# Batch normalisation with fixed statistics: even and odd channels as tiles, and transfers that no longer wait their turn

## The chip, the cores and the metric

The kernel runs on one core of a Trainium2 chip. The metric is the device time of one execution in microseconds (us); lower is better. The profile is of one such execution. Its span runs from the first to the last instruction, and is a little shorter than the device time.

## The reference

The input x has the shape 32 x 256 x 128 x 128 (images, channels, height, width) in float32. Each channel has a gamma, a beta, a mean and a variance, which are given:

```python
return gamma * (x - mean) / np.sqrt(var + eps) + beta
```

For each channel this is one multiplication and one addition per element, with scale = gamma / sqrt(var + eps) and shift = beta - mean * scale. The input is 536.87 MB, the output as much, and each element is used once.

## The kernel before

**Tiles.** An image has 256 channels and a tile has 128 partitions, so the work is 64 tiles (NT = 64), two per image: channels 0 to 127, then 128 to 255 (lines 40 and 41). A partition holds one channel of one image, 16,384 elements or 65,536 bytes, contiguous in HBM. A tile is 8 MiB, contiguous in HBM as well. Three buffers in SBUF, `bufs[0..2]`, take the tiles in turn, and a tile is computed in place.

**Loads.** SyncE (SP) issues all loads, in order, on one DMA queue (q1 in the profile). Tile 0 comes in two pieces: the left quarter of its columns (line 84), then four small loads of the parameters (line 87), then the other three quarters (line 91). For each later tile (lines 92 to 100), SyncE waits until the store that last used the buffer has landed (line 97). From tile 2 on it also waits until the load before has landed (line 100, attached to the instruction of line 98), and only then issues the load. So the load queue holds one transfer at a time.

**Parameters.** Each vector of 256 values is loaded into 16 partitions of `rows`. VectorE (DVE) transposes `rows` in blocks of 32 x 32 into `turned` (line 104), and four small copies (line 109) place the values in `par`, one channel per partition, with one column for each half of the channels. ScalarE (ACT) takes the square root (line 111), and VectorE computes `scale_t` and `shift_t` (lines 118 to 121). These are 128 x 2: column `i % 2` serves tile i.

**Compute.** One TENSOR_SCALAR of VectorE per tile (line 126) waits for the load and multiplies and adds in place. Tile 0 is computed in two pieces. The last tile is divided: VectorE takes its first 9216 columns, ScalarE the rest (line 154).

**Stores.** ScalarE issues all stores, in order, on a queue of its own (q10). Before store i it waits until store i - 1 has landed (`turn_of_store`, lines 140 and 141), and the store itself waits for the compute (line 138). So the store queue holds one transfer at a time too. The last store has no such wait for the one before. At the end SyncE waits for all stores (line 164).

SyncE, ScalarE and VectorE each work through their instructions in program order. An instruction that waits holds up all behind it on its engine.

Of the kernel before, what the change touches and what calls it, by code (L numbers as in the profile page):

```python
# [8 lines left out]
NBUF = 3  # L9
# [4 lines left out]
@with_exitstack  # L14
def kernel(
    ctx: ExitStack,
    tc: tile.TileContext,
    x: bass.AP,
    gamma: bass.AP,
    beta: bass.AP,  # L20
    running_mean: bass.AP,
    running_var: bass.AP,
    out: bass.AP,
):
    nc = tc.nc
    eps = 1e-5
    f32 = mybir.dt.float32

    N, C, H, W = x.shape
    P = nc.NUM_PARTITIONS  # L30
    assert C % P == 0
    NCB = C // P
    HW = H * W
    NT = N * NCB
    B = 32
    NQ = P // B
    NE = 16
    NPAR = 4

    xr = x.rearrange("n (cb p) h w -> (n cb) p (h w)", p=P)  # L40
    outr = out.rearrange("n (cb p) h w -> (n cb) p (h w)", p=P)

    params = ctx.enter_context(tc.tile_pool(name="params", bufs=1))
    data = ctx.enter_context(tc.tile_pool(name="data", bufs=1))
    bufs = [data.tile([P, HW], f32, name=f"t{s}", tag=f"t{s}") for s in range(NBUF)]
    rows = params.tile([B, NPAR * C], f32, name="rows", tag="rows")
    turned = params.tile([B, NPAR * C], f32, name="turned", tag="turned")
    par = params.tile([P, NPAR, NCB], f32, name="par", tag="par")
    eps_t = params.tile([P, 1], f32, name="eps_t", tag="eps")
    std_t = params.tile([P, NCB], f32, name="std_t", tag="std")  # L50
    rstd_t = params.tile([P, NCB], f32, name="rstd_t", tag="rstd")
    scale_t = params.tile([P, NCB], f32, name="scale_t", tag="scale")
    ms_t = params.tile([P, NCB], f32, name="ms_t", tag="ms")
    shift_t = params.tile([P, NCB], f32, name="shift_t", tag="shift")

    loaded = [tc.alloc_semaphore(f"loaded{s}") for s in range(NBUF)]
    stored = [tc.alloc_semaphore(f"stored{s}") for s in range(NBUF)]
    early = tc.alloc_semaphore("early")  # L60
    done = tc.alloc_semaphore("done")
    fetched = tc.alloc_semaphore("fetched")
    vec = tc.alloc_semaphore("vec")
    act = tc.alloc_semaphore("act")

    with tc.tile_critical():  # L66
        count = [0]

        def step(inst, sem=None, value=None):

            if sem is not None:
                inst._wait_ge(sem, value)
            elif count[0]:
                inst._wait_ge(vec, count[0])
            inst.then_inc(vec, 1)
            count[0] += 1
            return count[0]

        left, right = slice(0, HW // 4), slice(HW // 4, HW)
        last = NT - 1  # L80

        nc.sync.dma_start(out=bufs[0][:, left], in_=xr[0][:, left]).then_inc(early, 16)
        zeroed = step(nc.vector.memset(rows[:], 0.0))  # L85
        for r, ap in enumerate((running_var, gamma, beta, running_mean)):
            inst = nc.sync.dma_start(out=rows[0:NE, r * C : (r + 1) * C], in_=ap.partition_broadcast(NE))  # L87
            if r == 0:
                inst._wait_ge(vec, zeroed)
            inst.then_inc(fetched, 16)  # L90
        nc.sync.dma_start(out=bufs[0][:, right], in_=xr[0][:, right]).then_inc(loaded[0], 16)  # L91
        for i in range(1, NT):
            s, turn = i % NBUF, i // NBUF


            if turn:
                nc.sync.wait_ge(stored[s], 16 * turn)
            inst = nc.sync.dma_start(out=bufs[s][:], in_=xr[i]).then_inc(loaded[s], 16)
            if i >= 2:
                inst._wait_ge(loaded[(i - 1) % NBUF], 16 * ((i - 1) // NBUF + 1))  # L100


        step(nc.vector.memset(eps_t[:], eps))  # L103
        step(nc.vector.transpose(out=turned[:], in_=rows[:]), fetched, 16 * NPAR)  # L104

        blocks = turned.rearrange("p (rc q b) -> p rc q b", q=NQ, b=B)
        flat = par.rearrange("p r cb -> p (r cb)")
        for q in range(NQ):
            placed = step(nc.vector.tensor_copy(out=flat[q * B : (q + 1) * B], in_=blocks[:, :, q, 0]))  # L109
        var_t, gamma_t, beta_t, mean_t = (par[:, r] for r in range(NPAR))  # L110
        nc.scalar.activation(  # L111
            out=std_t[:],
            in_=var_t,
            func=mybir.ActivationFunctionType.Sqrt,
            bias=eps_t[:],
            scale=1.0,
        )._wait_ge(vec, placed).then_inc(act, 1)
        step(nc.vector.reciprocal(out=rstd_t[:], in_=std_t[:]), act, 1)  # L118
        step(nc.vector.tensor_mul(out=scale_t[:], in0=gamma_t, in1=rstd_t[:]))  # L119
        step(nc.vector.tensor_mul(out=ms_t[:], in0=mean_t, in1=scale_t[:]))  # L120
        ready = step(nc.vector.tensor_sub(out=shift_t[:], in0=beta_t, in1=ms_t[:]))  # L121
        nc.vector.wait_ge(vec, ready)

        def compute(i, cols=slice(0, HW)):
            t, cb = bufs[i % NBUF], i % NCB
            return nc.vector.tensor_scalar(  # L126
                out=t[:, cols],
                in0=t[:, cols],
                scalar1=scale_t[:, cb : cb + 1],
                scalar2=shift_t[:, cb : cb + 1],  # L130
                op0=mybir.AluOpType.mult,
                op1=mybir.AluOpType.add,
            ).then_inc(done, 1)

        def store(i, after):
            s = i % NBUF
            inst = nc.scalar.dma_start(out=outr[i], in_=bufs[s][:]).then_inc(stored[s], 16)
            inst._wait_ge(done, after)

        def turn_of_store(i):  # L140
            nc.scalar.wait_ge(stored[(i - 1) % NBUF], 16 * ((i - 1) // NBUF + 1))

        compute(0, left)._wait_ge(early, 16)
        compute(0, right)._wait_ge(loaded[0], 16)
        store(0, 2)
        for i in range(1, last):
            compute(i)._wait_ge(loaded[i % NBUF], 16 * (i // NBUF + 1))
            turn_of_store(i)
            store(i, i + 2)

        turns = last // NBUF + 1
        compute(last, slice(0, VCOLS))._wait_ge(loaded[last % NBUF], 16 * turns)
        t, cb = bufs[last % NBUF], last % NCB
        nc.scalar.activation(  # L154
            out=t[:, VCOLS:],
            in_=t[:, VCOLS:],
            func=mybir.ActivationFunctionType.Identity,
            bias=shift_t[:, cb : cb + 1],
            scale=scale_t[:, cb : cb + 1],
        )._wait_ge(loaded[last % NBUF], 16 * turns).then_inc(done, 1)  # L160
        store(last, last + 3)

        for s in range(NBUF):
            nc.sync.wait_ge(stored[s], 16 * ((NT - s + NBUF - 1) // NBUF))
# [30 lines left out]
```

## Time and profile before

| | us |
|---|---|
| median of 3 runs | 2488.96 |
| lowest, highest | 2486.43, 2489.02 |
| the profiled execution's own time | 2486.43 |
| its span | 2484.7 |
| VectorE busy | 564.0 |
| ScalarE busy | 7.9 |
| a load or a store of 8 MiB, from issue to landing | 38.6 |
| first store issued | 30.04 |
| last load landed, last store issued | 2454.41, 2460.82 |

All profile lines are from the profiled execution. A busy time is the time that an engine spent in instructions; waiting and issuing DMAs do not count. In a line of the chain of waits, the first number is the start in us from the start of the span, the second the length. "A <- B: total, times, longest" in a list of waits says that A stood for B, in us. In a group line, "8.31 <-DMA t<-in_x_dram" in brackets is the engine's idle time just before, and what ended it. DMA digits are tenths of the 16 DMA engines' time in 40 slices of the span, where 9 is 90% or more.

### The profile page before, as it was taken

What the parts mean: (1) busy time and instruction counts of PE and PEld (TensorE: products, weight loads), DVE (VectorE), ACT (ScalarE), POOL (GpSimd) and SP (SyncE); (2) the same over time, 40 slices, a digit from 0 to 9 for tenths busy, and PEclk for the clock granted to TensorE, in tenths of its full rate; (3) what the DMA queues carried; (4) which work ended last, traced back from release to release, by engine and by line L of the source; (5) the groups of instructions that cost most, each with busy time, mean ns of one, the idle gap of its engine ahead of it and who ended that gap; (6) DMA issues with size and microseconds to landing.
All of it is one profiled execution on the core that took longest, in us unless ns stands there. A gap on an engine that the chain in (4) does not pass through costs nothing.

```text
span 2484.7 us, 389 instructions
## 1 busy us (share of the span) xinstructions
DVE 564.0 (23%) x76; ACT 7.9 (0%) x3; POOL 0.2 (0%) x4
## 2 busy tenths in 40 slices
DVE  3121221212212222122221221212212122121221
ACT  0000000000000000000000000000000000000001
POOL 0000000000000000000000000000000000000000
DMA  9999999999999999999999999999999999999999
GB/s 422 423 439 434 430 436 435 437 428 437 435 436 432 433 438 429 436 434 431 434 427 437 437 426 439 436 432 430 436 438 430 433 427 438 430 430 437 436 426 406
DMA packets 18707, 1073.84 MB, mean 432 GB/s; under 512 B 2128, under 2 KB 2192, under 8 KB 2192
## 3 DMA queue, kind: packets, MB, share of 16 engines
q1 hardware_dynamic: 9488, 536.94, 50.1%
q10 hardware_dynamic: 9216, 536.88, 49.9%
q14 instruction: 3, 0.02, 0.0%
HBM read 536.94 MB, written 536.87 MB: 432 GB/s over the span
## 4 chain that ended last, share of the span: by engine, by line
DMA 99%; ACT 0%; SPq 0%; issue 0%; DVE 0%; DVEq 0%
DMA t<-in_x_dram 99%; ACT t L154 0%; SPq L87 0%; DVE rows L85 0%; SPq L91 0%; DVE eps_t L103 0%; DVEq L190 0%; SPq L66 0%
## 5 line engine op out<-in xcount | busy, mean ns | idle before, releaser
L126 DVE TENSOR_SCALAR t<-t,scale_t,shift_t 128x16384 f32<-128x16384 f32 (+2 forms) x65 | 560.5, 8624 | 1886.5 <-DMA t<-in_x_dram 1886.4
L154 ACT ACTIVATE t<-t,shift_t,scale_t 128x7168 f32<-128x7168 f32 x1 | 6.4, 6361 | 2442.7 <-DMA t<-in_x_dram 2442.7
L104 DVE STREAM_TRANSPOSE turned<-rows 32x1024 f32<-32x1024 f32 x1 | 1.2, 1233 | 7.1 <-DMA rows<-in_running_mean_dram 7.1
L111 ACT ACT_TABLE_LOAD x1 | 1.3, 1283 | 0.9 <-SPq L66 0.9
L85 DVE MEMSET rows<- 32x1024 f32 x1 | 0.9, 912 | 1.2 <-SPq L66 1.2
L109 DVE COPY par<-turned 32x8 f32<-32x8 f32 x4 | 0.6, 162 | 0.1
L111 ACT ACTIVATE std_t<-par,eps_t 128x2 f32<-128x2 f32 x1 | 0.3, 295 | 9.2 <-DVE par L109 9.2
L118 DVE RECIPROCAL rstd_t<-std_t 128x2 f32<-128x2 f32 x1 | 0.2, 166 | 0.4 <-ACT std_t L111 0.4
L121 DVE TENSOR_TENSOR shift_t<-par,ms_t 128x2 f32<-128x2 f32 x1 | 0.2, 163 | 0.0
L120 DVE TENSOR_TENSOR ms_t<-par,scale_t 128x2 f32<-128x2 f32 x1 | 0.2, 161 | 0.0
L119 DVE TENSOR_TENSOR scale_t<-par,rstd_t 128x2 f32<-128x2 f32 x1 | 0.2, 161 | 0.0
L179 POOL MEMSET const-bfloat16-1.0<- 128x1 bf16 x1 | 0.1, 102 | 0.0
L179 POOL MEMSET const-uint8-127<- 128x1 uint8 x1 | 0.1, 101 | 0.0
L179 POOL MEMSET const-float32-0.0<- 128x1 f32 x1 | 0.1, 99 | 0.2 <-issue 0.2
L179 POOL MEMSET const-float32-1.0<- 128x1 f32 x1 | 0.1, 98 | 0.0
L103 DVE MEMSET eps_t<- 128x1 f32 x1 | 0.1, 59 | 0.1
## 6 DMA issues: line engine op xcount, KB each, us to landing
t<-in_x_dram SPq DMA_DIRECT2D x1, 6144.0 KB, 19.4
t<-in_x_dram SPq DMA_DIRECT2D x1, 2048.0 KB, 7.6
out_dram<-t ACTq DMA_DIRECT2D x64, 38.6
t<-in_x_dram SPq DMA_DIRECT2D x63, 38.6
rows<-in_running_var_dram SPq DMA_DIRECT2D x1, 16.0 KB, 6.4
rows<-in_gamma_dram SPq DMA_DIRECT2D x1, 16.0 KB, 6.2
rows<-in_beta_dram SPq DMA_DIRECT2D x1, 16.0 KB, 5.9
rows<-in_running_mean_dram SPq DMA_DIRECT2D x1, 16.0 KB, 5.9
```

What stands on the lines that cost most here:

```text
L85: zeroed = step(nc.vector.memset(rows[:], 0.0))
L103: step(nc.vector.memset(eps_t[:], eps))
L104: step(nc.vector.transpose(out=turned[:], in_=rows[:]), fetched, 16 * NPAR)
L109: placed = step(nc.vector.tensor_copy(out=flat[q * B : (q + 1) * B], in_=blocks[:, :, q, 0]))
L111: nc.scalar.activation(out=std_t[:], in_=var_t, func=mybir.ActivationFunctionType.Sqrt, bias=eps_t[:], scale=1.0,)._wait_ge(vec, placed).t ...
L118: step(nc.vector.reciprocal(out=rstd_t[:], in_=std_t[:]), act, 1)
L119: step(nc.vector.tensor_mul(out=scale_t[:], in0=gamma_t, in1=rstd_t[:]))
L120: step(nc.vector.tensor_mul(out=ms_t[:], in0=mean_t, in1=scale_t[:]))
L121: ready = step(nc.vector.tensor_sub(out=shift_t[:], in0=beta_t, in1=ms_t[:]))
L126: return nc.vector.tensor_scalar(out=t[:, cols], in0=t[:, cols], scalar1=scale_t[:, cb : cb + 1], scalar2=shift_t[:, cb : cb + 1], op0=myb ...
L154: nc.scalar.activation(out=t[:, VCOLS:], in_=t[:, VCOLS:], func=mybir.ActivationFunctionType.Identity, bias=shift_t[:, cb : cb + 1], scale ...
L179: nc = _bacc.Bacc("TRN2", target_bir_lowering=False, num_devices=1)
```

## The change

Tile i now holds the even channels of an image (i even) or the odd ones (i odd), so partition p holds channel 2p or 2p + 1. The rows of a tile are 65,536 bytes as before, but lie 131,072 bytes apart in HBM, for loads and stores alike. The parameters follow: one more VectorE copy, of 32 x 1024 elements, puts the even channels before the odd ones in a new tile `lined`, which is transposed in place of `rows`.

The two rules of one transfer at a time are dropped. A load now waits only for the store that frees its buffer, and a store only for its compute. The three buffers, the split of the first and the last tile, the queues and the order of the issues stay.

```diff
-    xr = x.rearrange("n (cb p) h w -> (n cb) p (h w)", p=P)
-    outr = out.rearrange("n (cb p) h w -> (n cb) p (h w)", p=P)
+    xv = x.rearrange("n (p cb) h w -> n cb p (h w)", cb=NCB)
+    outv = out.rearrange("n (p cb) h w -> n cb p (h w)", cb=NCB)
+    xr = [xv[i // NCB, i % NCB] for i in range(NT)]
+    outr = [outv[i // NCB, i % NCB] for i in range(NT)]
...
+    lined = params.tile([B, NPAR * C], f32, name="lined", tag="lined")
...
+            inst = nc.sync.dma_start(out=bufs[s][:], in_=xr[i]).then_inc(loaded[s], 16)
             if turn:
-                nc.sync.wait_ge(stored[s], 16 * turn)
-            inst = nc.sync.dma_start(out=bufs[s][:], in_=xr[i]).then_inc(loaded[s], 16)
-            if i >= 2:
-                inst._wait_ge(loaded[(i - 1) % NBUF], 16 * ((i - 1) // NBUF + 1))
+                inst._wait_ge(stored[s], 16 * turn)
...
-        step(nc.vector.transpose(out=turned[:], in_=rows[:]), fetched, 16 * NPAR)
+        step(
+            nc.vector.tensor_copy(
+                out=lined.rearrange("b (r cb p) -> b r cb p", r=NPAR, cb=NCB),
+                in_=rows.rearrange("b (r p cb) -> b r cb p", r=NPAR, cb=NCB),
+            ),
+            fetched,
+            16 * NPAR,
+        )
+        step(nc.vector.transpose(out=turned[:], in_=lined[:]))
...
         def store(i, after):
             s = i % NBUF
-            inst = nc.scalar.dma_start(out=outr[i], in_=bufs[s][:]).then_inc(stored[s], 16)
-            inst._wait_ge(done, after)
-        def turn_of_store(i):
-            nc.scalar.wait_ge(stored[(i - 1) % NBUF], 16 * ((i - 1) // NBUF + 1))
+            nc.scalar.dma_start(out=outr[i], in_=bufs[s][:])._wait_ge(done, after).then_inc(stored[s], 16)
...
-            turn_of_store(i)
             store(i, i + 2)
```

## The prediction

> **What bounds the kernel now.** I read the shares of busy time first, then the DMA part, then the chain of work that ended last, then SyncE's own waits, and last the head and the tail in order of time.
>
> ```profile
> DVE 564.0 (23%) x76; ACT 7.9 (0%) x3; POOL 0.2 (0%) x4
> ...
> DMA  9999999999999999999999999999999999999999
> ...
> q1 hardware_dynamic: 9488, 536.94, 50.1%
> q10 hardware_dynamic: 9216, 536.88, 49.9%
> ...
> DMA 99%; ACT 0%; SPq 0%; issue 0%; DVE 0%; DVEq 0%
> ```
>
> VectorE is busy for less than a quarter of the span. The two DMA queues, loads on q1 and stores on q10, together took 50.1 + 49.9 = 100.0% of the time of the 16 DMA engines. So no engine ever stands still long enough to be seen, and the chain is 99% DMA. The question is therefore not whether a ring waits, but whether a DMA engine does.
>
> ```profile
> 247.22 38.65 DMA t<-in_x_dram
> ...
> 1214.33 38.80 DMA t<-in_x_dram
> ...
> 1253.15 39.06 DMA t<-in_x_dram
> ...
> 1601.49 39.35 DMA t<-in_x_dram
> ...
> 2377.15 38.62 DMA t<-in_x_dram
> ```
>
> These are pieces of the chain: start, length, what. One load of 8 MiB takes 38.6 us because a store of 8 MiB shares the engines with it. The shortest piece is 38.62. In the trace's packet records one row of 65,536 bytes takes 2.418 us, load or store, and an engine starts the next row 2.414 us after the last one. A tile and its store are 16 rows per engine, 16 x 2.414 = 38.62: the shortest piece is an engine that never pauses. Sixty-four such tiles cost 64 x 38.62 = 2471.7 us. The span of 2484.7 is only 13.0 above that. Of the 13.0, the periods between load 1 (landed at 52.87) and load 63 (landed at 2454.41, seen as the ACTIVATE's start at 2454.43) hold 2401.56 - 62 x 38.62 = 7.1 us. The rest is head (first row at about 2.0 us) and tail (last store landed at 2483.4).
>
> The 7.1 us lie in a few stretches, such as pieces of 38.80, 39.06 and 39.35. The packet records say whose they are: the load rows took 5.2 us per engine more than 2.418 each over the run, the store rows 0.1. So what this kernel still loses is mostly a slow read of HBM now and then, and not a ring without work.
>
> ```profile
> SPq L98 <- DMA t<-in_x_dram: 1378.8, 62, 48.0
> SPq L97 <- DMA out_dram<-t: 1009.0, 61, 16.8
> ```
>
> SyncE issues load i, then waits 1009.0 / 61 = 16.5 us for the store that frees the next buffer (line 97), then another 1378.8 / 62 = 22.2 us for load i itself to land (line 98), and issues load i+1.
>
> **The change, part by part.**
>
> *The load's wait for the load before goes (line 100 of before, shown under line 98).* Each load can then be issued when its buffer is free, some 22 us earlier, and lies in the load ring when the one before ends. Removed: 62 waits of 22.2 us of SyncE, whose only other work is the next issue (0.33 us each). What is late next is the wait for the store, and that is over 22 us before the load ring needs work. Gain on the path: in before, the load ring is empty for a moment at each change of load (from issue to first row; at the start the first issue is at 0.95 and the first row at 1.98, so about 1 us, or a little over a packet with the landing). But in this moment the store ring has the engine alone and moves two of its rows in the time of one (the last store, alone, takes 19.3 us where 38.6 is the rule). The engine loses nothing, and the store gets back later what it lent. So the gain is 0. If this cover were gone (both rings empty at once), a gap would cost about 1 us, 62 of them 62 us; the 100.0% rules that out in before, and the chain's own excess of 7.1 us bounds it.
>
> *The store's wait for the store before goes (line 141, turn_of_store).* A load lands, its compute takes 8.81 us, and the store before lands 16.5 us after the load. So the store is issued 16.5 - 8.8 = 7.7 us earlier and lies queued. Behind it on ScalarE's queue there are only later stores, and the last tile's ACTIVATE, which waits for its load. By the same reasoning the gain is 0.
>
> *Both rings now always hold work.* Loads run at 38.62 per tile, and buffers come free in time: load i+3 needs store i, which lands 16.5 us after load i+1, or 22 us before load i+2 ends. The order of the two streams stays as it is, so the tail does too: store 62 is still moving when the last compute ends (now 2460.8; the engines work throughout), and the last store goes alone for 19.3 us. Change: 0.
>
> *Parameters: one more VectorE copy.* The copy of 32x1024 with a stride of two elements is not in the trace. Below, the 32x1024 MEMSET took 0.91 us; above, I take two of the STREAM_TRANSPOSE of that shape, 2 x 1.23 = 2.5 us. I take 1.2, the single transpose, which also reads and writes 1024 elements. All of it delays the first compute, which has this cover:
>
> ```profile
> 12.61 2.41 DVE L126 TENSOR_SCALAR t<-t,scale_t,shift_t 128x4096 f32<-128x4096 f32 x1
> 23.33 6.68 DVE L126 TENSOR_SCALAR t<-t,scale_t,shift_t 128x12288 f32<-128x12288 f32 x1 [8.31 <-DMA t<-in_x_dram]
> ```
>
> VectorE stands 8.31 us before the second piece of tile 0 lands. Even 2.5 us goes into it: cost 0. The cover would have to shrink below 2.5 for the copy to move store 0 (30.04). The four parameter loads are issued as before.
>
> *Rows 128 KiB apart instead of 64 KiB.* Each partition still reads or writes 65,536 contiguous bytes, one packet, so packet count and size stay the same: 128 rows for each transfer. SBUF's side is unchanged. In HBM a tile is now every second row of 16 MiB. The trace shows no such pattern, so I bound it by the rows there are. Lowest: all excess goes, 62 periods of 38.62, -7.1 us. Highest: each period is like the worst piece, 39.35 against the present mean of 2401.56 / 62 = 38.735, so 62 x 0.615 = +38 us. Between them lies the stretch at 1136 to 1292 us (38.88, 39.01, 38.80, 39.06; mean 38.94), 62 x 0.20 = +12.6 us. I take 0, since the nearest row is the present load itself: same packet, same engines, and 99 of 100 packets at 2.418.
>
> The Trainium skill speaks against this edit: the page "DMA: Bandwidth & Descriptors", section "Latency and other measured facts", says that copies whose per-partition rows lie a large power of two apart in HBM lose rate, 207 GB/s each way at 512 KiB against 214 at full rate, and far less from 2 MiB up. By its figure for 512 KiB the sum would be 214 / 207 = 1.034 times the time, an estimate of some 2570 us; the page has no figure for 128 KiB, and the trace of before, at 64 KiB, shows about 217 each way (8.39 MB in 38.65 us), no loss.
>
> **Sum.** Load ring 0, store ring 0, tail 0, copy 0, row distance 0 (-7.1 to +38). Against the profiled execution (2486.43, span 2484.7) that is 2486.4. This execution is the lowest of the three shown, whose median is 2488.96, 0.1% above; I place the forecast between the two, at 2488.
>
> **Rivals.**
>
> *No change (the forecast), chance 0.60.* The rings are never empty and the engines as full as before. For it: 100.0% and the 38.62 floor. It covers 2484 to 2494, the median +- 0.2% (about what a measurement of this kernel can tell from no change).
>
> *Slower by reads of HBM, chance 0.26.* The place is the load packet, which already has nearly all of the lengthening (5.2 against 0.1 us per engine). If the wider rows make the slow stretch the rule, 38.94 per tile, the time is 2488 + 12.6 = 2501; if all are like the worst piece, 2526. It decides from a mean period of 38.735 + 5 / 62 = 38.82 on. For it: the slow stretches involve most engines at once, so they come from something that the engines share (the records show up to 16 load rows lengthened within 3 us). Against it: each row is still read as one contiguous packet, and most periods show no trace of a limit.
>
> *Faster, chance 0.14.* The wider rows, or the rings that run without pause, take the slow stretches away: 2488 - 7.1 = 2481. For it: nothing in the trace says that 64 KiB is the best distance for reads. Against it: the waits removed do not coincide with the slow stretches, which come at irregular times. Less than 2480 would need rows faster than 2.414 us, which the trace never shows.
>
> *The change does not do what it says.* If stores landed too late, loads would still go out only as the one before lands, and the time would be 2488 as well; the 22 us speak against it. This is inside the first case.
>
> Left out at the top are the slow cases beyond 2503, about 1 in 10, and at the bottom 1 in 30. So the range is 2480 to 2503; the likeliest case alone has 2484 to 2494.
>
> **What would show it.** SyncE's waits should show one line, for stores, and no longer a wait for the load before. Issue to landing of a load should rise from 38.6 to about 38.6 + 22 = 61 us without the kernel being slower, since part of it is queueing; that of a store to about 46. VectorE's idle time before the second piece of tile 0 should fall to about 7. The sum of the two queues should stay at 100%, and the pieces between loads at 38.62 to 38.7. I am wrong if pieces of 38.9 or more are the rule (reads), if the sum of the queues falls under 99% (a ring without work), or if the last store no longer starts with the engines busy.

## The result, and the profile after

| | before | after |
|---|---|---|
| median of 4 runs each, same chip, us | 2487.69 | 2508.43 |
| lowest, highest | 2485.97, 2489.02 | 2507.63, 2509.33 |
| the profiled execution, its span | 2486.43, 2484.7 | 2507.63, 2505.8 |
| last load landed | 2454.41 | 2475.11 |
| last store issued, landed | 2460.82, 2483.39 | 2481.52, 2504.09 |

The changed kernel is slower: the ratio is 1.0084, with a 95% interval of 1.0066 to 1.0101. The forecast was no change, at 2488, with a range to 2503. The runs of some kernels below (waits at every second tile, three passes, two pieces with waits) fall into a faster and a slower group, so for these the spread is given, and for the first two the ratio leaves out the slowest runs.

The table already says where the time is. The last load lands 20.70 us later. From there on the two kernels are alike: 6.41 us to the issue of the last store in both, and 22.57 us to its landing in both. So the whole loss is in the date of the last load. The page of the kernel after:

```profile
GB/s 420 432 432 430 431 426 435 433 432 433 434 433 434 433 433 433 433 430 426 431 433 432 425 434 433 434 430 427 434 435 430 425 434 434 433 424 433 433 433 320
...
q1 hardware_dynamic: 9488, 536.94, 49.9%
q10 hardware_dynamic: 9216, 536.88, 49.6%
...
another core or an unknown queue 75%; DVE 22%; DMA 2%; ACT 0%; issue 0%; SPq 0%; ACTq 0%; DVEq 0%
...
out_dram<-t ACTq DMA_DIRECT2D x64, 49.7
t<-in_x_dram SPq DMA_DIRECT2D x63, 58.5
```

Three lines matter. The queues sum to 99.5% instead of 100.0%: 0.5% of 2505.8 is 12.5 us per engine without a packet. The last slice moved 320 GB/s, where before it was 406. And the chain no longer says DMA 99%. The rates of the kernel before, for the last slice:

```profile
GB/s 422 423 439 434 430 436 435 437 428 437 435 436 432 433 438 429 436 434 431 434 427 437 437 426 439 436 432 430 436 438 430 433 427 438 430 430 437 436 426 406
```

That the chain follows "another core or an unknown queue" here only means that a load was issued long before the wait that it ends, so the profile ties nothing to it; one core runs. A load takes 58.5 us from issue to landing and a store 49.7, both mostly queueing. SyncE's own waits in the kernel after:

```profile
SPq L98 <- DMA out_dram<-t: 2390.5, 61, 67.1
SPq L167 <- DMA out_dram<-t: 67.9, 1, 67.9
```

The wait for the load before is gone, as the diff says. In the order of time, the end of the kernel after:

```profile
2435.92 8.81 DVE L134 TENSOR_SCALAR t<-t,scale_t,shift_t 128x16384 f32<-128x16384 f32 x1 [29.90 <-DMA t<-in_x_dram]
2475.13 6.36 ACT L157 ACTIVATE t<-t,shift_t,scale_t 128x7168 f32<-128x7168 f32 x1 [2462.62 <-DMA t<-in_x_dram]
...
2481.52 0.34 ACTq L145 DMA_DIRECT2D out_dram<-t  x1
```

Around these, stretches of the kernel after (start and end, length, busy times, then clock, DMA share and GB/s):

```profile
2455.00:2467.00 12.00, 0.00 (x0) 0.00 (x0) 0.00 (x0) 1.00 1.01 437
2467.00:2469.00 2.00, 0.00 (x0) 0.00 (x0) 0.00 (x0) 1.00 0.31 131
2469.00:2482.00 13.00, 5.08 (x1) 6.36 (x1) 0.00 (x0) 1.00 0.27 116
2482.00:2504.00 22.00, 0.00 (x0) 0.00 (x0) 0.00 (x0) 1.00 0.89 384
```

and the same place of the kernel before, its last compute and the stretch after it:

```profile
2449.00:2461.00 12.00, 5.08 (x1) 6.36 (x1) 0.00 (x0) 1.00 1.01 437
2461.00:2463.50 2.50, 0.00 (x0) 0.00 (x0) 0.00 (x0) 1.00 0.98 419
```

Before, the DMA engines are full while the last tile is computed, and still full when the last store is issued. After, their share is 0.27 for 13 us, during the last compute and before it. A share of 0.27 is about 4 of 16 engines. So 12 engines have ended all their work and wait, and 4 still carry the last load.

**One landing is sixteen.** The profile's "landing" of a transfer is the last of 16 events in the trace, one for each DMA engine. The Trainium skill, page "DMA: Bandwidth & Descriptors", section "Why a DMA increments its semaphore by 16 and not by 1", says that the engines of a transfer finish independently and that each adds one; the trace agrees, with 16 records for each transfer of this kernel. Their spread in us, from the first engine to the last, worked out from these records for a load of the same number in four kernels (the last two are experiments told below; "landed at" is the time in the kernel before):

```
load   landed at   before   after   even/odd only   free rings only
   4       170       1.0     2.3         3.8              0.6
  10       402       4.0     7.5         4.2              1.5
  19       750       4.2    17.2         4.3             14.1
  25       982       4.3    21.8         4.3             23.2
  31      1214       1.2    27.3         4.5             27.0
  43      1680       4.7    26.8         4.3             27.0
  63       end       4.8    27.1         4.0             26.8
engines over 10 us late at the end
                     0       4           0                1
```

In the kernel after, four engines fall behind, slowly at first, until they are 27 us behind the others. There it stops. The 12 others are not late: the first engines end the last load at 2448.0, before at 2449.6. But compute needs all 16. Of the 20.70 us, 15.6 are lost by load 31, when the lag has reached 27 us (it lands at 1229.87, before at 1214.31), and 5.1 after it.

The 20.7 us can be split. Summed from the packet records, a mean engine is busy for 2482.6 us before and 2492.4 after: +9.8, of which the load rows are +5.0 (their lengthening over 2.418 us per row goes from 5.2 to 10.2) and the store rows +4.7 (0.1 to 4.8). The rest is idle: 12 engines for 13.4 to 15.4 us before the last store, 12 x 14.4 / 16 = 10.8. Together 20.6. That is the mean of 16 engines. Strung together row by row, the records show no engine with a pause of more than 0.6 us until these 12 stop; the four late ones never stop, so what they lose is longer rows alone.

The head, which the prediction also touched, in the kernel after:

```profile
9.45 0.68 DVE L104 COPY lined<-rows 32x1024 f32<-32x1024 f32 x1 [7.21 <-DMA rows<-in_running_mean_dram]
...
23.31 6.68 DVE L134 TENSOR_SCALAR t<-t,scale_t,shift_t 128x12288 f32<-128x12288 f32 x1 [7.49 <-DMA t<-in_x_dram]
30.02 71.00 ACTq L145 DMA_DIRECT2D out_dram<-t  x3
```

The copy took 0.68 us, the idle time behind it fell from 8.31 to 7.49, and the first store was issued at 30.02 (before 30.04): it is hidden.

### The profile page after: what moved, and what is told of

Its sections match the earlier page's. It is cut to its first block, busy times and chain, and to the rows that moved or that the text cites. A ratio compares the mean times of both kernels' runs of the same rounds, so it can differ in the third digit from the quotient of the medians.

```text
span 2505.8 us, 267 instructions
## 1 busy us (share of the span) xinstructions
DVE 564.7 (23%) x77; ACT 7.9 (0%) x3; POOL 0.2 (0%) x4
## 4 chain that ended last, share of the span: by engine, by line
another core or an unknown queue 75%; DVE 22%; DMA 2%; ACT 0%; issue 0%; SPq 0%; ACTq 0%; DVEq 0%
DVE t L134 22%; DMA t<-in_x_dram 2%; ACT t L157 0%; SPq L91 0%; DVE rows L89 0%; SPq L95 0%; ACTq L145 0%; DVE eps_t L102 0%; DVEq L193 0%; SPq L70 0%
## 6 DMA issues: line engine op xcount, KB each, us to landing
t<-in_x_dram SPq DMA_DIRECT2D x1, 6144.0 KB, 19.4
out_dram<-t ACTq DMA_DIRECT2D x64, 49.7
t<-in_x_dram SPq DMA_DIRECT2D x63, 58.5
```

## The experiments

The expectations speak of theories by letters. **A**: rows 131,072 bytes apart are read more slowly. **B**: the two waits kept the 16 DMA engines in step; without them an engine that loses time stays behind and loses more. **D**, formed later: the lag is bounded by the room in the three buffers, and this bound is the price. **F**, later too: the length of the row decides whether a lag arises. Each ratio is to the kernel before, run in turn with it on the same chip. "Lengthening" is the time by which the rows of an engine exceed the usual row, summed over the run, as a mean of 16 engines.

### Each part of the change alone

**The even and odd tiles with both waits put back:**

```diff
+                nc.sync.wait_ge(stored[s], 16 * turn)
+            inst = nc.sync.dma_start(out=bufs[s][:], in_=xr[i]).then_inc(loaded[s], 16)
+            if i >= 2:
+                inst._wait_ge(loaded[(i - 1) % NBUF], 16 * ((i - 1) // NBUF + 1))
...
+            turn_of_store(i)
             store(i, i + 2)
```

> The changed kernel with both one-transfer-at-a-time waits put back: only the even and odd channels remain of the change. Theory A (rows 128 KiB apart in HBM make the reads, and some writes, slower): about 2508 us, load rows lengthened by about 10 us per engine and store rows by about 5, as in the changed kernel. Theory B (with no wait for the transfer before, some DMA engines fall behind the others, and the end waits for them): about 2488 us, lengthening 5 and 0.1 as before the change, and the 16 landings of one load within 5 us. Theory C (both are needed together): 2488 us here and in the run with free rings alone.

Measured: 2484.67 (2482.55 to 2489.83), ratio 0.9999 (0.9990 to 1.0009). The page and the chain of this kernel:

```profile
q1 hardware_dynamic: 9488, 536.94, 50.1%
q10 hardware_dynamic: 9216, 536.88, 49.9%
...
DMA 99%; ACT 0%; SPq 0%; issue 0%; DVE 0%; DVEq 0%
```
```profile
2336.89 38.61 DMA t<-in_x_dram
...
2375.51 38.63 DMA t<-in_x_dram
...
2414.16 38.61 DMA t<-in_x_dram
```

The periods are at the floor of 38.62, with rows 131,072 bytes apart. A is dead, and so is the copy as a cause.

**The channels as before, both waits taken out** (the kernel before, with the waits of loads and stores as in the kernel after):

```diff
-            if i >= 2:
-                inst._wait_ge(loaded[(i - 1) % NBUF], 16 * ((i - 1) // NBUF + 1))
...
-            turn_of_store(i)
             store(i, i + 2)
```

> The kernel before with both one-transfer-at-a-time waits taken out and the lower and upper half of the channels kept: rows 64 KiB apart. Theory A: about 2488 us, and the landings of one load at most 5 us apart. Theory B: about 2508 us, with some engines' landings up to 27 us behind the others. Theory C: 2488 us.

Measured: 2505.76 (2504.42 to 2506.84), ratio 1.0079 (1.0061 to 1.0098). The whole loss is here. Its page, and its stretches early, late, and while the last tile is waited for and computed:

```profile
q10 hardware_dynamic: 9216, 536.88, 49.7%
q1 hardware_dynamic: 9488, 536.94, 49.7%
```
```profile
100.00:300.00 200.00, 44.48 (x6) 0.00 (x0) 0.00 (x0) 1.00 1.00 435
2300.00:2420.00 120.00, 26.44 (x3) 0.00 (x0) 0.00 (x0) 1.00 0.99 428
...
2469.00:2481.00 12.00, 5.08 (x1) 6.36 (x1) 0.00 (x0) 1.00 0.06 27
```

A DMA share of 0.06 is one engine of 16 (1/16 = 0.0625): here a single engine carries the last load, and the landing records say the same. Up to about 340 us nothing lags (spread 0.6, period 38.64 to 38.68), although a store here lands 19.3 us after a load and in the kernel before 16.9: while the engines are in step, that distance costs nothing. Then this engine falls behind: the last landings of loads 12 to 21 come 38.9 to 40.8 us apart, 39.8 on average, while those of the first engine come 38.62 to 38.65 apart up to load 18. Most of it is in the first load row after the late engine's own landing. From load 28 on, 27 us behind, it loses nothing more against the others, but all engines together still lose a little: the period is 38.87 on average, in the kernel before 38.76 over the same loads. B says this much: the lag is not caught up, and it grows.

**The same kernel once more:**

> The kernel with free rings alone once more, for a second profile. If the lag belongs to certain engines or to chance alone, its size at the end would differ; if buffers stop it, some engines, be it one or several, are again 27 us behind at the end, and the time is again about 2506 us.

Measured: 2503.55, one run. One engine begins to lag at about 670 us instead of 400, a second follows it, and the lag reaches the same stop (26.7 us at load 41, which lands at 1615.62 us, and 27.4 at most later). When it began and how many engines lagged differed from run to run; where it ended did not.

### One wait at a time

**Stores free, the load's wait put back:**

```diff
+                nc.sync.wait_ge(stored[s], 16 * turn)
+            inst = nc.sync.dma_start(out=bufs[s][:], in_=xr[i]).then_inc(loaded[s], 16)
+            if i >= 2:
+                inst._wait_ge(loaded[(i - 1) % NBUF], 16 * ((i - 1) // NBUF + 1))
```

> The changed kernel with the load's wait for the load before put back; stores stay free. Theory A: about 2508 us, since the rows lie apart as in the changed kernel. Theory B: 2488 us if the loads are the ring in which engines run ahead, since no engine can start load i+1 before all have ended load i; 2508 us if it is the stores.

Measured: 2507.95 (2504.16 to 2512.65), ratio 1.0089 (1.0067 to 1.0112). As slow as the change, but in another way: the 16 landings of a load stay within 5.2 us. Computes in the order of time in this kernel:

```profile
1033.38 8.81 DVE L136 TENSOR_SCALAR t<-t,scale_t,shift_t 128x16384 f32<-128x16384 f32 x1 [32.26 <-DMA t<-in_x_dram]
1070.27 8.81 DVE L136 TENSOR_SCALAR t<-t,scale_t,shift_t 128x16384 f32<-128x16384 f32 x1 [28.07 <-DMA t<-in_x_dram]
1111.32 8.81 DVE L136 TENSOR_SCALAR t<-t,scale_t,shift_t 128x16384 f32<-128x16384 f32 x1 [32.24 <-DMA t<-in_x_dram]
1147.74 8.81 DVE L136 TENSOR_SCALAR t<-t,scale_t,shift_t 128x16384 f32<-128x16384 f32 x1 [27.61 <-DMA t<-in_x_dram]
```

The same place in the kernel before:

```profile
1020.47 8.81 DVE L126 TENSOR_SCALAR t<-t,scale_t,shift_t 128x16384 f32<-128x16384 f32 x1 [29.85 <-DMA t<-in_x_dram]
1037.40 155.24 ACTq L137 DMA_DIRECT2D out_dram<-t  x5
1059.09 8.81 DVE L126 TENSOR_SCALAR t<-t,scale_t,shift_t 128x16384 f32<-128x16384 f32 x1 [29.80 <-DMA t<-in_x_dram]
```

There the periods are 38.6 to 38.7 with few exceptions, and a store, issued when the one before has landed, goes out 16.9 us after a load lands. With free stores the periods alternate, 36.9, 41.1, 36.4. The stores have run ahead until they wait for the compute: they land 7.2 and 12.0 us after a load in turn. After a landing at 7.2 us the compute of 8.81 us still runs, so the next store begins in an empty ring on all 16 engines at once. The load rows take 22.5 us per engine longer over the run (before 5.2); the largest part, 9.1 us, lies 10 to 12.5 us after a load lands, where these stores begin.

**Loads free, the store's wait put back:**

```diff
+        def turn_of_store(i):
+            nc.scalar.wait_ge(stored[(i - 1) % NBUF], 16 * ((i - 1) // NBUF + 1))
...
+            turn_of_store(i)
             store(i, i + 2)
```

> The changed kernel with the store's wait for the store before put back; loads stay free. Theory A: about 2508 us. Theory B: 2508 us if engines run ahead in the load ring, 2488 us if in the store ring.

Measured: 3209.94 (3208.14 to 3216.89), ratio 1.2918 (1.2890 to 1.2945). No theory had this. Its page and one tile in the order of time:

```profile
q1 hardware_dynamic: 9488, 536.94, 47.9%
q10 hardware_dynamic: 9216, 536.88, 40.9%
```
```profile
1023.32 8.81 DVE L134 TENSOR_SCALAR t<-t,scale_t,shift_t 128x16384 f32<-128x16384 f32 x1 [42.43 <-DMA t<-in_x_dram]
1023.48 52.51 SPq L98 DMA_DIRECT2D t<-in_x_dram  x2
1023.54 52.53 ACTq L145 DMA_DIRECT2D out_dram<-t  x2
1075.50 8.81 DVE L134 TENSOR_SCALAR t<-t,scale_t,shift_t 128x16384 f32<-128x16384 f32 x1 [43.36 <-DMA t<-in_x_dram]
```

From about 205 us on a load and a store land 0.2 us apart, and the next load and the next store are issued within 0.06 us of each other. Both wait for the same landing: the load for the store that frees its buffer, the store for the store before it. Both rings are then empty at the same moment, which the prediction had priced at about 1 us a tile. The price is far more, about 51 us a tile instead of 38.6: the engines idle for (100 - 88.8)% of 3209.3 = 359 us, and load and store rows that start together take longer, 299 and 74 us per engine. The engines are in step here too, 8.1 us apart at most. So either wait alone keeps the engines together, but moves the landing of a store towards that of a load: 16.9 us after it in the kernel before, 7.2 and 12.0 in turn with the load's wait alone, 0.2 with the store's. The two waits together held the distance at 16.9; how much of the loss is due to the distance itself and how much to rows that start together was not separated.

### How often the waits are needed

**Both waits at every eighth tile, at every second tile, and only from tile 32 on** (the kernel with both waits, under a condition; the first of the three):

```diff
-            if i >= 2:
+            if i % 8 == 0:
                 inst._wait_ge(loaded[(i - 1) % NBUF], 16 * ((i - 1) // NBUF + 1))
...
+            if i % 8 == 0:
-            turn_of_store(i)
+                turn_of_store(i)
```

The others have `i % 2 == 0` and `i >= 32` in its place.

> The changed kernel (even and odd channels) with both waits for the transfer before put back at every 8th tile only. Theory B1 (an engine that lags loses more because it lags, so the lag must be cut from time to time): the lag has 8 tiles to grow, less than 5 us at first, so the landings of one load stay within some 8 us and the time is about 2490 us. Theory B2 (the lag only shows a loss that an engine has at any rate while its rings hold more than one transfer): 7 of 8 tiles lose as in the changed kernel, about 2505 us. Theory B3 (only a ring's own phase against the other matters, as in the kernels with one ring free): between the two, with store landings not at a fixed distance from load landings.

> As the run with the waits at every 8th tile, but at every 2nd. Theory B1: at most 2488 us, as with all waits. Theory B2: half the loss, about 2496 us. Theory B3: other than both if the distance of store to load landings leaves 17 us.

> The changed kernel with both waits put back from tile 32 on; tiles 1 to 31 are free. Theory B1 and B2: in the changed kernel the lag is at 27 us by then, that loss is not paid back, since the lagging engines never stood idle: about 2505 us, with the leading engines idle once, at the first waits. Rival (the cost arises at the end alone, where the last store waits for the lagging engines): the waits draw the engines together before the end, about 2488 us.

Every eighth: 2519.43 (2513.53 to 2526.30), ratio 1.0146 (1.0126 to 1.0165), slower than without any. At the tiles with waits the period is 41.5 to 43.5 us, of which the next tile gives only a part back, and from there on a lag of 7 to 19 us stays. Every second: median 2499.77, runs from 2484.30 to 2571.73, ratio 1.0042 (1.0017 to 1.0067) without the three runs above 2554; in the profiled run (2507.32) the store lands about 14 and 17 us after the load in turn, and the periods alternate, about 36 and 42. From tile 32 on: 2514.67 (2510.54 to 2519.66), ratio 1.0130 (1.0113 to 1.0148). Here load 31 lands 16.4 us later than in the kernel before (1230.75 against 1214.31), with the lag at 27 us. At tile 32 the waits cut it to 11, at periods of 43.2, 40.2, 40.1 and 39.4 us; by load 36 another 8.1 us are lost, and none of it is given back. So the loss is not an end effect that is paid with the last tile: most of it is there when the lag has grown, and returning to step costs more.

### Which stream makes the lag

**Loads alone** (leaves out all stores but the last; loads wait only for the compute that frees the buffer) and **stores alone** (leaves out the loads of tiles 3 to 63; a compute waits for the store that last used the buffer), each as an edit of the kernel after:

```diff
-                inst._wait_ge(stored[s], 16 * turn)
+                inst._wait_ge(done, i - NBUF + 2)
...
-            store(i, i + 2)
```
```diff
-        for i in range(1, NT):
+        for i in range(1, NBUF):
...
-            compute(i)._wait_ge(loaded[i % NBUF], 16 * (i // NBUF + 1))
+            inst = compute(i)
+            if i < NBUF:
+                inst._wait_ge(loaded[i], 16)
+            else:
+                inst._wait_ge(stored[i % NBUF], 16 * (i // NBUF))
```

> Leaves out the stores of all tiles but the last, so that most of the output is not written; load i waits for the compute of tile i - 3 in place of a store. Loads run free in their ring. If the lag needs loads and stores side by side (theory B1 or B2 with mixed traffic): the landings of one load stay within 1 us of each other, the load rows are not lengthened, and the time is 64 x 19.31 + 19.3 + 6.4 + about 5, or some 1267 us. If reading alone makes engines lag: landings several us apart, and over 1275 us.

> Leaves out the loads of tiles 3 to 63: each buffer is computed again in place after its store, so the output is not the reference's. Stores run free in their ring, as in the changed kernel, with rows of 65,536 bytes. If the lag needs loads and stores side by side: landings of a store within 1 us, store rows not lengthened, 64 x 19.31 + 30 + 5, about 1271 us. If stores alone make engines lag: landings several us apart and a longer time.

Loads alone: 1274.03, 19.35 us per tile, spread 1.2 us at most, lengthening 1.9. Stores alone: 1307.88, 19.36 us per store, spread 1.2 at most once the three loads are in, lengthening 3.0; the expectation had left out the three loads at the start, which are the difference. Their queues, of loads alone and then of stores alone:

```profile
q1 hardware_dynamic: 9488, 536.94, 97.6%
q10 hardware_dynamic: 144, 8.39, 1.5%
```
```profile
q10 hardware_dynamic: 9216, 536.88, 95.1%
q1 hardware_dynamic: 704, 25.23, 4.6%
```

A free ring by itself keeps its 16 engines in step for the whole run. The lag needs both streams.

### Rows and pieces

**Half tiles** (8192 columns, rows of 32,768 bytes, 128 tiles), with three or six buffers, with both waits or free:

```diff
-    HW = H * W
-    NT = N * NCB
+    NCH = 2
+    HW = H * W // NCH
+    NT = N * NCB * NCH
```

> The kernel before (lower and upper half of the channels, both waits) with tiles of half a row: 8192 columns, 128 tiles, three buffers of 32,768 bytes per partition, so half the bytes in buffers. It is the control for the next run. All theories: landings of one load within about 3 us, 19.3 us per half tile, about 2490 us.

> The same with both waits taken out. Theory D (the lag grows until the buffers stop it; the stop is three tile times less a load, a compute and a store: 115.9 - 38.6 - 8.8 - 38.6 = 30 us less some 3 us of issue and landing, 27 us, with whole rows): here the stop is 57.9 - 19.3 - 4.4 - 19.3 - 3 = 12 us, so the landings of one load end up 12 us apart and the time is some 8 us over its control, instead of 21. Rival theory E (the lag stops at 27 us for another reason, such as the number of rows): the lag is 27 us or 12 rows again, 15 to 21 us over its control.

> The same half tiles and waits with six buffers, so the bytes in buffers of the kernel before. Control for the next run. All theories: as the control with three buffers, about 2490 us.

> Six half buffers, both waits taken out. Theory D: the stop is 6 x 19.3 - 19.3 - 4.4 - 19.3 - 3 = 70 us, so the lag may grow past 27 us over the whole run; at the 0.6 to 1.9 us per 38.6 us seen in tiles 12 to 25 of the run with free rings alone it reaches 30 to 70 us, and the time is 25 us or more over its control. Rival theory E: the lag stops at 27 us, about 21 us over its control.

| half tiles | median (lowest to highest) | ratio (interval) | largest spread | lengthening load, store |
|---|---|---|---|---|
| 3 buffers, waits | 2504.34 (2495.61 to 2509.00) | 1.0060 (1.0040 to 1.0080) | 7 | 7.0, 10.0 |
| 3 buffers, free | 2488.19 (2488.11 to 2488.36) | 1.0004 (0.9995 to 1.0014) | 3.5 | 1.0, 0.1 |
| 6 buffers, waits | 2495.52 (2492.51 to 2510.81) | 1.0052 (1.0031 to 1.0072) | 4.1 | 5.3, 0.2 |
| 6 buffers, free | 2488.31 (2488.15 to 2488.67) | 1.0005 (0.9996 to 1.0014) | 2.2 | 1.3, 0.1 |

The spread is the largest of any load or store in the profiled run. The sign turns round. With half tiles the free rings do not lag, and it is the waits that cost, 16.2 and 7.2 us. Since no lag arose, these runs say nothing on what bounds it (D). The queues of three buffers, free:

```profile
q1 hardware_dynamic: 18704, 536.94, 50.1%
q10 hardware_dynamic: 18432, 536.88, 50.0%
```

They sum to 100.1%, as full as in the kernel before, without any wait of one transfer for another.

**Whole tiles, each load and store issued as two transfers of half the columns**, rows of 32,768 bytes, three whole buffers, free and with both waits:

```diff
-            inst = nc.sync.dma_start(out=bufs[s][:], in_=xr[i]).then_inc(loaded[s], 16)
+            inst, _ = [nc.sync.dma_start(out=bufs[s][:, c], in_=xr[i][:, c]).then_inc(loaded[s], 16) for c in halves]
```

> The kernel with free rings and lower and upper half of the channels, whole tiles and three whole buffers as there, but each load and each store issued as two transfers, the left and the right half of the columns, so that a row in the DMA rings is 32,768 bytes. Theory F (the length of a row decides whether a lag grows: engines take a row of each ring in turn, and with rows of 65,536 bytes one that is out of step loses more): as with half tiles and free rings, the landings of a load within 4 us, load rows lengthened by about 1 us per engine in all, about 2488 us. Theory G (the smaller tile, with its shorter compute and its other order of HBM addresses, stops the lag): as the kernel with free rings, lag to 27 us, about 2505 us.

> As the run before, but with both waits for the whole transfer before. Theory F: 2488 to 2500 us, as the half tiles with waits; the waits gain nothing here, or lose. Theory G: 2488 us, as the kernel before.

Free: 2681.64 (2680.02 to 2688.32), ratio 1.0799 (1.0784 to 1.0815). Its queues:

```profile
q10 hardware_dynamic: 18432, 536.88, 48.9%
q1 hardware_dynamic: 18704, 536.94, 46.7%
```

The rows are as short as in the half tiles, and the lag is there early: 10 us at 202 us. From about 350 us on up to two engines land a first piece some 22 us and a second piece some 34 us after the others, and the period is 42 us. The store rows are 68 us longer per engine, the load rows 11. F is refuted: the row's length alone does not decide. The expected times were missed too. With waits: one run at 2491.39 and three at 2539.21 to 2552.62. The profiled one is of the upper three and has load rows 52.5 us longer per engine; with the runs so far apart nothing is concluded from this kernel.

### What bounds the lag

**Two and three passes of compute** (one or two TENSOR_SCALAR more per tile, times 1 plus 0; a tile is computed for 17.6 or 26.5 us instead of 8.8), free rings:

```diff
+            for k in range(1):
+                inst = nc.vector.tensor_scalar(
+                    out=t[:],
+                    in0=t[:],
+                    scalar1=one_t[:],
+                    scalar2=zero_t[:],
...
+            compute(i)._wait_ge(mid, i * 1)
```

> The kernel with free rings and lower and upper half of the channels, with the compute of tiles 1 to 62 made longer: a first pass of VectorE multiplies by 1 and adds 0, so 17.6 us in place of 8.8 from landing to store. Theory D (the lag stops where the leading engines run out of work: they have stored and loaded all that they may, and the next store waits for the lagging engine's load and the compute; stop = 38.6 - compute - some 3 us, 27 us so far): the landings of a load end up 38.6 - 17.6 - 3 = 18 us apart, and the time is about 9 us shorter than with free rings and one pass, 2495 to 2497 us, although VectorE does twice the work. Theory H (the lag stops at 27 us for another reason, or each tile loses some time whatever the lag): 27 us again and 2505 us or more.

> The same with three passes, 26.5 us from landing to store. Theory D: stop at 38.6 - 26.5 - 3 = 9 us, time about 2488 us. Theory H: 27 us and 2505 us or more.

Two passes: 2528.23 (2522.28 to 2544.77), ratio 1.0186 (1.0150 to 1.0222); the lag stops at 19 to 20.5 us for most of the run (23.7 at most). Three passes: median 2509.01, five runs at 2494.64 to 2496.94 and five at 2521.07 to 2533.11, ratio 1.0090 (1.0051 to 1.0130) without the two slowest; in the profiled run, which is of the upper five (2532.61), the lag stops at 9 to 11 us. D is right on the bound: with 8.8, 17.6 and 26.5 us of compute it is 27, 19.4 and 10.7, which is 38.6 less the compute less 1.4 to 2.8. It is wrong on the price: with two passes the lag is smaller and the loss twice as large. Three passes show both, a smaller loss in the lower five runs, of which there is no trace, and a larger one in the upper five.

The traces say where the larger loss lies. With two passes, load 8, where the lag has come near its stop, lands 7.6 us later than in the kernel before, and the last load 57.9; with three passes load 5 lands 7.0 us later and the last load 40.9. So here most is lost after the lag has stopped, where in the kernel after it was 5.1 of 20.7. In the profiled run of two passes the load rows are 21 us longer per engine and the store rows 32, of three passes 12 and 35. In the kernel after, the store rows lengthen only from about 1160 us on, when the lag has stopped. In all three the longer store rows lie where the compute has ended and the next store begins: 97% of the lengthening is 9.5 to 12.5 us after a load lands in the kernel after, 81% at 17 to 20.5 us with two passes, 97% at 26 to 30 us with three. In the records of the kernel with free rings alone, 12 engines take one load row after the other between 2014.6 and 2019.4 us, with no store row between; then the 12 begin their next store within 0.34 us of each other, and these rows take 2.71 to 3.15 us instead of 2.418. So at the bound the engines that are ahead have no store left and get the next one at the same moment. That rows take longer because they start together fits all of this, but it was not tried by itself.

## Why the prediction was wrong, point by point

**What bounds the kernel: right.** The engines are full, a tile is 38.62 us at best, and the kernel with even and odd tiles and both waits runs at 38.61 to 38.64 in the lines shown.

**"The engine loses nothing, and the store gets back later what it lent. So the gain is 0." This step failed**, and with it the store's "By the same reasoning the gain is 0". Removing both waits costs 20.96 us (2505.76 against the 2484.80 of before in that call), with nothing else changed. The step counted a wait as dead time: it asked what the ring loses while it stands empty, found nothing, and gave the wait no other effect. What the runs show in its place is that the waits were a meeting point. A load was issued only when all 16 engines had landed the one before, so an engine that had lost time began the next load with the others, 4.8 us apart at most. Without both waits, one, two or four engines fell behind by 27 us. The bound of 7.1 us that I set was a bound on gains from the present pieces, and I used it as if it also limited the loss.

**"Both rings now always hold work", "the engines work throughout", "Change: 0": wrong by the same failure.** It holds until the engines that are ahead have nothing left: once the lag has stopped, their store ring is empty for a part of each tile (in the packet records about three load rows follow directly on a load row then, per engine and tile, where in step it is one), and their share of the last 13 us before the last store is gone. The text itself named this sign: the last store no longer starts with the engines busy. The sum of the queues is 99.5%, above the 99% that I had named as the other sign, so that threshold was too coarse for a loss of 0.8%.

**Copy: 0, right**, with 0.681 us in place of 1.2, below my lower bound of 0.91 as well. The MEMSET of that shape was no lower bound.

**Row distance: 0, right.** The ratio is 0.9999 (0.9990 to 1.0009). The Trainium skill's row in "DMA: Bandwidth & Descriptors", "Latency and other measured facts", gives a loss from 512 KiB on. At 128 KiB the run here shows none, and no run here has wider rows. One reading behind the 0 was too smooth: not 99 of 100 load rows took 2.418 us in the kernel before, but 94 (of the store rows 99); nothing rests on it.

**Named signs.** SyncE has one line of waits: right. Issue to landing about 61 and 46: 58.5 and 49.7. VectorE's idle time about 7: 7.49. **The slower rival** had the sign and, at 2501 to 2526, the size, but by luck; its mechanism fell: it put the loss on reads of wider rows, and those cost nothing. The rival that I should have had is an engine out of step, and the trace of before held its sign: the 16 landings of one load, 0.6 us apart at 52.85, were up to 4.8 apart later and came no further.

**What stays open.** Why the load rows of an engine that is out of step take longer is not in any record; only that it needs both streams is shown. Nor do the records name the engines, so whether it is always the same ones is not known. Why half tiles with free rings don't lag, while two pieces per tile lag at once, is open. So is what sets the price once the lag has stopped, where D failed. None of these versions beats the kernel before; the even and odd tiles with both waits equal it, and so do the half tiles with free rings.

## What to carry to other kernels

A wait that costs no time where it stands can still set the distance between two streams and hold the 16 DMA engines of a transfer together, as these two did; when DMA is full, ask of each such wait what it keeps in step, not only what it delays. Look at the landings engine by engine and not at the last one, and try the removal with nothing else changed. Measure each wait of such a pair apart and both together, and again when the size or number of transfers changes: here the same removal cost 0.8% with whole tiles, nothing with half tiles, and one wait of the two alone cost 0.9% or 29%.

## What was unexpected of the hardware

- With loads and stores side by side and no wait between transfers, one DMA engine of 16 ran 27 us behind the others for 1300 us, while with one stream alone the landings of a transfer were at most 1.2 us apart.
- Loads and stores that begin at the same moment on all engines took about 51 us per tile, where the same bytes take 38.6 when a store lands 16.9 us after a load.
- Rows can take longer where a store begins in an empty ring on all engines: in the kernel before, the 16 load rows (starts 32.03 to 32.49 us) between the issue of the first store at 30.04 us and its first row at 35.00 take 0.2 to 0.8 us longer each. It is no rule: there each later store but the last begins in an empty ring as well, and the load rows take only 5.2 us longer per engine over the whole run.
- Two transfers of half the columns in place of one, with rows of 32,768 bytes, cost 8% with free rings (2681.64 us); the same rows as transfers of their own tiles cost nothing (2488.19).
